# Two-layer hybrid diffusion block on one core: latent chains ahead of context chains, one convolution channel as fp32 diagonal products in idle stretches, two group norms at a time, a gradual weight split

## The chip, the cores and the metric

The kernel runs on one core of a Trainium2 chip. The metric is the device time of one execution in microseconds, median of three runs. The engines are TensorE (PE; PEld is its weight load), VectorE (DVE), ScalarE (ACT), GpSimd (POOL) and the queue that issues transfers (SP). Each engine works off its own queue in order; they meet by semaphores.

## The reference, cut to what matters

Two layers over 256 latent tokens of width 1024, with 256 context tokens in the first layer only. All of it is fp32.

```python
for i in range(2):
    x_lat = x_lat + 0.5 * post(swiglu(pre(x_lat, m, 0, g0), w_gu, w_down), m, 0, g1)
    if i == 0: x_ctx = the same for the context
    if i == 0:                                   # even mixer
        u = pre(x_lat, m, 1, g2) @ w_in
        a = silu(groupnorm(dw_conv31(u_a * sigmoid(u_g)) + b))     # 512 channels, 8 groups
        q, k, v = ...                            # 8 heads of 64
        b = softmax([q k_window + bias, q k_ctx]) @ [v_window, v_ctx]
        y = [a, b] @ w_out
    else:                                        # odd mixer
        b, c, z = split(pre(x_lat, m, 1, g2) @ w_in, 3)
        y = (b * dw_conv3(c * z)) @ w_out
    x_lat = x_lat + post(y, m, 1, g3)
    x_lat = x_lat + 0.5 * post(swiglu(pre(x_lat, m, 2, g4), w_gu2, w_down2), m, 2, g5)
pre(x, m, k, g)  = rms_norm(x, g) * (1 + m[3k+1]) + m[3k]
post(y, m, k, g) = m[3k+2] * rms_norm(y, g)
m = silu(c) @ w_mod + b                          # 9 rows of 1024 per layer
```

## The kernel before, in words

**Weights.** Every weight streams once through SBUF. A raw chunk arrives by one of SP's transfers (`load`, tile `wr`, four buffers), ACT rounds a piece of 128x512 to the TensorE's reduced fp32 (`cast`, the high half of `wx`), DVE subtracts for the low half (`feed`), and each product is three matmuls: high by high, high by low, low by high (`mm3`, `rows3`). A ring of 12 slots (`RING`), later 15, holds split pieces; some pages (`lent`) serve as further slots for the last products of a stage. `wtile` hands out a piece and splits `feedst["auto"]` pieces ahead: `LEAD` (6) as a rule and `DEEP` before a tail.

**Stages.** `ff1_0` works on latents and context together, 512 tokens wide, in five parts (`PARTS0`). The other feed-forward stages (`half_step` for `ff2_0`, `ff1_1`, `ff2_1`) work on 256 latents: 22 pairs of gate and up, 48 matmuls each, then the down projection in `Out`. Between them stand the even mixer (`ev_in`, `ev_out`) and the odd one (`od_in`, `od_out`).

**Order.** The queues are written out by hand: after `pin[0] = True` every instruction stays where it was emitted. A planner carries a clock for PE, DVE and ACT (`clk`, `cost_pe` and so on). Chains of work are generators started by `spawn`; each yields the clock at which it wants to go on, and `tick`, called with each weight piece, lets those that are due emit. `need(cond)` moves PE's clock on to the next due chain until the condition holds. `filler` emits weight splits, or taps of the convolution, where ACT or DVE is not far ahead of PE.

**Modulation rows.** DVE makes most of `m` as 128 rows of dot products (`mod_dot`, tile `junk`, one instruction each per condition); POOL loads each row (`mod_load`, tile `mr`) into one of three or four pages when the dot product before it has freed the page. `bg(n)` emits n of them.

**End of the first stage.** After each of four token tiles of the last down part a chain `chain0(t)` normalises the row, updates the residual, normalises again, transposes in four quarters on PE and splits the result in two halves for `ev_in` (`hla` for the latents t = 0 and 1, `hct` for the context t = 2 and 3). Each chain is started as soon as its tile is done.

**Even mixer.** `ev_in` makes four convolution channels tiles and q from the latents, then v of all tokens (waits for the context's chains), then k. The convolution's 31 taps run on DVE for channel tiles 0 to 2 (`taps`, tile `bufD`); tile 3 runs on PE as products with diagonal matrices in the split form, three matmuls a tap (`taps_pe`), each step of k followed by one tap (`next(tap_pe, None)`). POOL lays the diagonals (`lay`, two instructions a tap, a ring of four). `groups` normalises the tiles one after the other: matmuls for mean, variance and spread, and a power on POOL. `unit(n)` is one half of a pair of heads of the attention: scores, a bias that POOL has loaded and negated (`bias_load`, tile `bt`, DMA and multiply emitted together), softmax, transposes, and the product with v. `ev_out` takes its eight k tiles in `EV_ORDER`; the last four (`EV_TAIL`) form its tail.

**`Out`.** It accumulates two token tiles in four PSUM banks, leaves the last `tail` k tiles to the end, tile by tile, and for each token tile a `chain(t)` normalises, updates the residual, multiplies by the next scale row on POOL (`PO.tensor_mul`), normalises, transposes and splits into `hin`; `head` starts the next stage tile by tile while the other chain still runs. The chains of both tiles emit by due time; the first square of each is emitted right after its first bank.

## Time and profile before

| | before |
|---|---|
| median of three runs | 1312.34 us (1312.02 to 1313.12) |
| the profiled execution's own time | 1318.65 us |
| its span in the profile | 1316.9 us |
| PE busy | 1234.2 us (94%), 7321 matmul records |
| DVE / ACT / POOL busy | 884.8 / 583.8 / 181.5 us |
| mean granted TensorE clock | 0.966 |
| HBM | 259.74 MB read, 198 GB/s over the span |

The profile is of one execution. Busy time counts an engine's instructions as a union over time; PE at half its clock is busy for twice as long with the same work, so idle time and granted clock are read together. Fp32 matmuls show as two records each. All work of the pinned part has the line of the helper that emits it (L110), so groups are told apart by tiles.

### The profile page before, as it was taken

What the parts mean: (1) busy time and instruction counts of PE and PEld (TensorE: products, weight loads), DVE (VectorE), ACT (ScalarE), POOL (GpSimd) and SP (SyncE); (2) the same over time, 40 slices, a digit from 0 to 9 for tenths busy, and PEclk for the clock granted to TensorE, in tenths of its full rate; (3) what the DMA queues carried; (4) which work ended last, traced back from release to release, by engine and by line L of the source; (5) the groups of instructions that cost most, each with busy time, mean ns of one, the idle gap of its engine ahead of it and who ended that gap; (6) DMA issues with size and microseconds to landing.
All of it is one profiled execution on the core that took longest, in us unless ns stands there. A gap on an engine that the chain in (4) does not pass through costs nothing.

```text
span 1316.9 us, 19547 instructions
## 1 busy us (share of the span) xinstructions
PE 1234.2 (94%) x7321; PEld 1081.7 (82%) x7321; DVE 884.8 (67%) x1681; ACT 583.8 (44%) x1209; POOL 181.5 (14%) x273
## 2 busy tenths in 40 slices
PE   7999999999996978876999999999998899999997
PEld 4788888888875967754999987999987897899986
DVE  5868787776464765473677776677867687676562
ACT  5542323222357514453455455444545345454451
POOL 0001011211010046502000102100102001100000
PEclk9999999999996988997999999999998989999999
DMA  8846466885321611150588894678984467476670
GB/s 323 323 144 217 166 221 227 286 289 180 103 102 40 217 49 60 57 173 16 199 281 272 313 331 141 222 266 272 321 308 145 144 194 254 165 252 197 195 262 34
DMA packets 73895, 262.13 MB, mean 199 GB/s; under 512 B 8188, under 2 KB 10436, under 8 KB 73800
## 3 DMA queue, kind: packets, MB, share of 16 engines
q1 hardware_dynamic: 52440, 183.74, 40.4%
q0 software_dynamic: 21360, 77.14, 18.1%
q8 instruction: 57, 0.93, 0.3%
q14 instruction: 38, 0.31, 0.1%
HBM read 259.74 MB, written 1.11 MB: 198 GB/s over the span
## 4 chain that ended last, share of the span: by engine, by line
PE 42%; DVE 6%; DMA 6%; ACT 3%; issue 1%; POOL 0%; DVEq 0%; POOLq 0%; ACTq 0%; SPq 0%
PE mm L110 40%; DMA wr<-in_wflow 6%; DVE wx L110 2%; PE bc L110 2%; DVE junk L110 1%; DVE yw L110 1%; ACT wx L110 1%; ACT ajunk L110 1%; DVE xt L110 1%; DVE xn L110 0%; DVE gh L110 0%; DVE uu L110 0%; ACT hin L110 0%; DVE hin L110 0%; ACT gs L110 0%
## 5 line engine op out<-in xcount | busy, mean ns | idle before, releaser
L110 DVE TENSOR_TENSOR wx<-wr,wx 128x512 fp32r<-128x512 f32 x648 | 417.9, 691 | 76.0 <-ACT wx L110 75.7
L110 ACT CAST wx<-wr 128x512 fp32r<-128x512 f32 x648 | 365.6, 618 | 196.1 <-DMA wr<-in_wflow 141.8
L110 PE MATMUL mm<-hin,wx 128*128 128x256 f32 x3168 | 385.1, 284 | 3.6 <-DVE wx L110 3.6
L110 PEld LDWEIGHTS mm<-hin,wx 128*128 128x128 f32 x3168 | 383.6, 193 | 3.8 <-DVE wx L110 3.8
L110 PE MATMUL mm<-hh,wx 128*128 128x512 f32 x704 | 220.2, 392 | 1.8 <-ACT hh L673 1.3
L110 DVE SCALAR_TENSOR_TENSOR junk<-mr,cb 128x1024 bf16<-128x1024 f32 x156 | 190.0, 1218 | 0.3
L110 PEld LDWEIGHTS mm<-hh,wx 128*128 128x128 f32 x704 | 132.9, 189 | 30.5 <-ACT hh L673 1.8
L110 POOL DMA_DIRECT2D mr<-in_wmodb x128 | 69.0, 539 | 571.5 <-DVE junk L110 524.1
L110 PE MATMUL mm<-hl,wx 128*128 128x512 f32 x352 | 137.4, 390 | 0.0
L110 PE MATMUL mm<-wx,Hh 128*128 128x512 f32 x352 | 108.8, 390 | 0.0
L110 DVE TENSOR_TENSOR gh<-gs,mm 128x256 f32<-128x256 f32 (+2 forms) x93 | 43.7, 474 | 95.4 <-ACT gs L110 55.5
L110 ACT ACTIVATE gs<-mm 128x256 f32<-128x256 f32 (+2 forms) x91 | 38.7, 429 | 133.3 <-PE mm L110 133.3
L110 PE MATMUL mm<-wx,hin 128*128 128x256 f32 (+1 forms) x384 | 80.7, 363 | 7.4 <-ACT hin L110 6.3
L110 PEld LDWEIGHTS mm<-wx,hin 128*128 128x128 f32 x384 | 61.7, 201 | 19.5 <-ACT hin L110 8.3
L110 PEld LDWEIGHTS mm<-hl,wx 128*128 128x128 f32 x352 | 66.4, 189 | 13.7
L110 PEld LDWEIGHTS mm<-wx,Hh 128*128 128x128 f32 x352 | 65.8, 188 | 13.7 <-DVE wx L110 0.2
L110 PE MATMUL mm<-hla,wx 128*128 128x256 f32 x384 | 61.5, 307 | 12.7 <-ACT hla L110 11.8
L110 PEld LDWEIGHTS mm<-hla,wx 128*128 128x128 f32 x384 | 54.3, 207 | 18.2 <-ACT hla L110 13.3
L110 PE MATMUL mm<-wx,Hl 128*128 128x512 f32 x176 | 68.6, 390 | 0.0
L110 PE MATMUL mm<-wx,Hb 128*128 128x512 f32 x288 | 67.2, 389 | 0.0
L110 PEld LDWEIGHTS mm<-wx,Hb 128*128 128x128 f32 x288 | 54.1, 188 | 11.2
L110 ACT CAST Hh<-gh 128x512 fp32r<-128x512 f32 x22 | 13.6, 620 | 108.8 <-DVE gh L110 108.8
(195 smaller groups left out, 1195.4 us busy)
## 6 DMA issues: line engine op xcount, KB each, us to landing
wr<-in_wflow SPq DMA_DIRECT2D x324, 512.0 KB, 5.5
mr<-in_wmodb POOLq DMA_DIRECT2D x128, 512.0 KB, 5.7
mr<-in_wmoda SPq DMA_DIRECT2D x8, 512.0 KB, 8.3
wme<-in_wmoda SPq DMA_DIRECT2D x8, 512.0 KB, 7.7
pr<-rowh POOLq DMA_DIRECT2D x7, 512.0 KB, 8.9
xt<-in_xtok SPq DMA_DIRECT2D x4, 512.0 KB, 3.9
bt<-in_bias POOLq DMA_DIRECT2D x4, 512.0 KB, 4.1
pr<-rowev POOLq DMA_DIRECT2D x3, 512.0 KB, 3.8
```

The costliest lines, as they stand in the source:

```text
L110: ins = f(*a, **kw)
```

## The change

1. `chain0` of a context tile waits until both latent tiles are through; its first square is one instruction of 1024 and its scaled copy two of 512 in place of four of 256.
2. Channel tile 0 in place of 3 goes to PE, as one fp32 matmul a tap and one diagonal on POOL, in a ring of eight. The taps no longer stand in the k loop: `need` calls them when no chain is due within 0.3 of PE's planned clock. DVE has tiles 1 to 3. `EV_ORDER` has tile 1 in front of tile 0.
3. Two `groups` generators run side by side.
4. `bias_load` is a chain: the transfer, 7 later the negation in two halves; a unit does not begin before its bias is there. The first load is emitted ahead of the v products. The row `M0` for `ev_out` is asked for when channel 0 is done, and the tail waits for all three rows.
5. In `Out`, chain 1 begins when chain 0 has emitted its second multiply, squares are emitted when their bank is full by the planner, the second multiply goes from POOL to DVE, and the first two transposes share a step.
6. The split ahead of a tail grows from 7 to 22 pieces by one a step (before: 6, then 18 for the last four), with three more lent pages (`M1` to `M3`); in `od_in` it grows from 6 to 14. The 16 modulation rows done beside those products move to `ff1_0`.

```diff
...
 PARTS0 = (4, 4, 4, 5, 5)
-EV_ORDER = (6, 4, 5, 0, 1, 2, 3, 7)
+EV_ORDER = (6, 4, 5, 1, 0, 2, 3, 7)
 EV_TAIL = 4
 LEAD = 6
-DEEP = 18
+DEEP = 22
 BACK = 1.2
...
     filler = [None]
+    idle_pe = [None]
...
                 return
+            if idle_pe[0] and min(x[0] for x in tasks) > clk["pe"] + 0.3 and idle_pe[0]():
+                tick()
+                continue
             clk["pe"] = max(clk["pe"], min(x[0] for x in tasks))
...
-        def __init__(self, name, base, src, K, tail, rows_, out_t=None, fill=None, lend=4, dots=0):
+        def __init__(self, name, base, src, K, tail, rows_, out_t=None, fill=None, lend=("A0", "A1", "A2", "A3", "M1", "M2", "M3")):
             self.rows, self.out_t = rows_, out_t
                                                  (K - tail) * KD + (n * tail + k - K + tail) * 4), 4)
-            lent.update({first + n: f"A{n}" for n in range(lend)})
+            lent.update({first + n: tag for n, tag in enumerate(lend)})
             self.y = y = [[take() for _ in range(2)] for _ in range(2)]
             for k in range(K - tail):
-                feedst.update(hold=(offs[name] * NTILE + base + k * KD) // 4, auto=DEEP if k >= K - tail - 4 else LEAD)
+                feedst.update(hold=(offs[name] * NTILE + base + k * KD) // 4, auto=max(feedst["auto"], min(DEEP, DEEP + 1 - K + tail + k)))
                 for t in range(2):
                         rows3(y[t][n], src(k), k, TS[t], w(k, n), k == 0, False)
-                bg(1 if k % 2 == 0 and k // 2 < dots else 0)
             feedst["hold"] = first
             filler[0] = fill or more
-            need(lambda: self.rows)
+            need(lambda: len(self.rows) == (1 if out_t else 3))
+            self.filled, self.mark = [0, 0], 0
             for t in range(2):
-                gen = self.chain(t)
+                spawn(self.chain(t), True)
                 for n in range(2):
                         rows3(y[t][n], src(k), k, TS[t], w(k, n), False, k == K - 1)
-                    if n == 0:
-                        next(gen)
-                spawn(gen, True)
+                    self.filled[t] = n + 1
                 feedst.update(hold=None, auto=0, at=first)
...
             for n in range(2):
+                while self.filled[t] <= n or self.mark < t:
+                    yield clk["pe"] + 0.2
                 square(ss, n, y[n])
             r = rstd(ss)
+            if self.out_t is not None:
+                self.mark = 1
             yield clk["dv"] + POW
             for n in range(2):
-                PO.tensor_mul(yw[:, half(n)], x[:, half(n)], a[:, half(n)])
+                DV.tensor_mul(yw[:, half(n)], x[:, half(n)], a[:, half(n)])
+            self.mark = 1
             yield both() + 0.1
...
             for c0, c1 in ((0, 2), (2, 4), (4, 8)):
-                while not free:
+                while len(free) < (2 if c0 == 0 else 1):
                     yield clk["pe"] + 0.2
-                pt = take("bc")
-                for k in range(c0, c1):
-                    PE.transpose(pt[:, (k - c0) * P:(k - c0 + 1) * P], yw[:, k * P:(k + 1) * P], ident)
+                pts = [take("bc")] if c0 != 2 else pts[1:]
+                if c0 == 0:
+                    pts.append(take("bc"))
+                pt = pts[0]
+                for p, e0, e1 in ((pts[0], 0, 2), (pts[1], 2, 4)) if c0 == 0 else ((pt, 4, 8),) if c0 == 4 else ():
+                    for k in range(e0, e1):
+                        PE.transpose(p[:, (k - e0) * P:(k - e0 + 1) * P], yw[:, k * P:(k + 1) * P], ident)
                 pv = pt[:, :(c1 - c0) * P].rearrange("p (q t) -> p q t", t=P)
...
                 self.ready[t] = c1
-                yield clk["pe"] + 0.3
+                if c0 == 2:
+                    yield clk["pe"] + 0.3
...
                           ("M0", "Y2", "Y3")[:3 if pre else 1])
-        return Out(name, NF * 16, H, NF, TAIL, rs, out_t, dots=8)
+        return Out(name, NF * 16, H, NF, TAIL, rs, out_t)
...
     feed(feedst["at"] + 1 + LEAD)
-    mod_begin(24 + 32 + 8, ("M0", "M1", "M2", "M3"))
+    mod_begin(24 + 32 + 24, ("M0", "M1", "M2", "M3"))
     parts = PARTS0
...
         a, b = pre[t // 2]
+        while t > 1 and min(kq[:2]) < KD:
+            yield clk["pe"] + 0.2
         ss = small.tile([P, 2], F32, name="ss")
-        for n in range(2):
-            clk["ac"] = both()
-            square(ss, n, y[:, half(n)])
+        clk["ac"] = both()
+        square(ss, 0, y)
         for n in range(2):
         yield both() + 0.1
-        r = rstd(ss)
+        r = rstd(ss[:, 0:1])
         yield clk["dv"] + POW
         for n in range(4):
-            c = slice(n * S, (n + 1) * S)
-            AC.activation(y[:, c], x[:, c], AF.Copy, scale=r)
-            yield clk["ac"] + 0.1
+            if n % 2 == 0:
+                AC.activation(y[:, half(n // 2)], x[:, half(n // 2)], AF.Copy, scale=r)
+                yield clk["ac"] + 0.1
             while not free:
...
                             k == 0, k == KD - 1)
-                        nd = (4, 5, 5, 4, 4 if f < 2 else 0)[pi]
+                        nd = (4, 5, 5, 5, 2 if f < 2 else 0)[pi]
                         bg(((gu * KD + k + 1) * nd) // 16 - ((gu * KD + k) * nd) // 16)
...
                 give(y[n])
-            if not last:
-                bg(1)
+            if not last and t:
+                bg(2)
             if last:
...
     acc = bufD[:, 2048:3072].rearrange("p (c t) -> p c t", t=S)
-    av = big.tile([P, 3, PADW], F32, name="av", tag="F")
+    avs = [big.tile([P, n, PADW], F32, name="av", tag=tag) for n, tag in ((3, "F"), (1, "M0"))]
+    av = [avs[1][:, 0, :]] + [avs[0][:, i, :] for i in range(3)]
...
     def taps():
-        for i in range(3):
+        for i in range(1, CT):
             for d in range(TAPS):
                     yield False
-                src = av[:, i, d:d + S]
+                src = av[i][:, d:d + S]
                 if d == 0:
...
-    diag = big.tile([P, 4, 2, P], F32R, name="diag", tag="R12")
+    diag = big.tile([P, 8, P], F32, name="diag", tag="R12")
     laid = []
         if d < TAPS:
-            PO.tensor_scalar(diag[:, d % 4, 0, :], ident, taph[:, d:d + 1].bitcast(F32), None, op0=ALU.mult)
-            PO.tensor_scalar(diag[:, d % 4, 1, :], ident, tapl[:, d:d + 1], None, op0=ALU.mult)
-            laid.append(max(laid[-1] if laid else 0, clk["pe"]) + 1.0)
+            PO.tensor_scalar(diag[:, d % 8, :], ident, dwh[:, 0, d:d + 1], None, op0=ALU.mult)
+            laid.append(max(laid[-1] if laid else 0, clk["pe"]) + 0.8)
     def taps_pe():
-        for _ in range(4):
+
+        for _ in range(8):
             lay()
-        yield
         ps = take()
         for d in range(TAPS):
-            w = diag[:, d % 4]
-            for u, v in ((0, 0), (0, 1), (1, 0)):
-                PE.matmul(ps[:, :S], lhsT=w[:, u, :], rhs=avp[:, v, d:d + S], start=d + u + v == 0,
-                          stop=d == TAPS - 1 and u == 1, skip_group_check=True)
+            while laid[d] > clk["pe"]:
+                yield False
+            PE.matmul(ps[:, :S], lhsT=diag[:, d % 8, :], rhs=av[0][:, d:d + S], start=d == 0, stop=d == TAPS - 1)
             lay()
-            if d == TAPS - 1:
-                AC.activation(acc[:, 3, :], ps[:, :S], AF.Identity, bias=dv[:, 0, 3:4])
-                give(ps)
-                st_["conv"].add(3)
-            yield
+            yield True
+        AC.activation(acc[:, 0, :], ps[:, :S], AF.Identity, bias=dv[:, 0, 0:1])
+        give(ps)
+        st_["conv"].add(0)
...
-        for n in range(CT):
-            while not (st_["conv"] - normed) or not turned():
+        while len(normed) < CT:
+            if not (st_["conv"] - normed) or not turned():
                 yield clk["pe"] + 0.5
+                continue
             i = min(st_["conv"] - normed)
...
         i, t = divmod(n, 2)
-        while st_["k"] <= i or st_["begun"] < n or st_["done"] < n - 1 or len(free) < 2:
+        while i not in bts or st_["k"] <= i or st_["begun"] < n or st_["done"] < n - 1 or len(free) < 2:
             yield clk["pe"] + 0.2
...
         if t == 1 and i + 1 < CT:
-            bias_load(i + 1)
+            spawn(bias_load(i + 1))
         if t == 1 and i >= 2:
...
     def bias_load(i):
-        bts[i] = page("bt", f"M{2 + i % 2}", [P, 2, 2, S])
-        PO.dma_start(out=bts[i], in_=bias[i])
-        PO.tensor_scalar(bts[i], bts[i], -1.0, None, op0=ALU.mult)
+        bt = page("bt", f"M{2 + i % 2}", [P, 2, 2, S])
+        PO.dma_start(out=bt, in_=bias[i])
+        yield clk["pe"] + 7
+        for m in range(2):
+            PO.tensor_scalar(bt[:, m], bt[:, m], -1.0, None, op0=ALU.mult)
+            yield clk["pe"] + 1
+        bts[i] = bt
     filler[0] = mixer_fill
-    spawn(groups())
+    for _ in range(2):
+        spawn(groups())
     for i in range(CT):
...
         AC.activation(th, ps[:, S:], AF.Tanh, scale=0.5)
-        if i < 3:
-            DV.scalar_tensor_tensor(av[:, i, PADT:PADT + S], th, 1.0, ps[:, :S], op0=ALU.add, op1=ALU.mult)
-        else:
-            avp = page("avp", "M0", [P, 2, PADW], F32R)
-            pad(avp.bitcast(F32))
-            a2, (ah, al) = work.tile([P, S], F32, name="full"), (avp[:, u, PADT:PADT + S] for u in range(2))
-            DV.scalar_tensor_tensor(a2, th, 1.0, ps[:, :S], op0=ALU.add, op1=ALU.mult)
-            AC.copy(ah, a2)
-            DV.tensor_sub(al, a2, ah.bitcast(F32))
+        DV.scalar_tensor_tensor(av[i][:, PADT:PADT + S], th, 1.0, ps[:, :S], op0=ALU.add, op1=ALU.mult)
         give(ps)
...
         give(ps)
+    spawn(bias_load(0))
     for t in range(4):
...
     mixer_pages()
-    bias_load(0)
     for n in range(2 * CT):
...
                     k == 0 and v == 0, k == KD - 1, True)
-            next(tap_pe, None)
         AC.copy(kT[:, i, :], ps)
         give(ps)
+        idle_pe[0] = lambda: next(tap_pe, False)
         st_["k"] = i + 1
-    ev_rows.insert(0, row_of(ev_vec[0], 0, "M0"))
+    def first_row():
+        while 0 not in st_["conv"] or len(ev_rows) < 2:
+            yield clk["pe"] + 0.5
+        ev_rows.insert(0, row_of(ev_vec[0], 0, "M0"))
+
+    spawn(first_row())
-    post = Out("ev_out", 0, src, KD, EV_TAIL, ev_rows, None, mixer_fill, 3)
+    post = Out("ev_out", 0, src, KD, EV_TAIL, ev_rows, None, mixer_fill, ("A0", "A1", "A2"))
     slots[:0] = ["X2", "X3", "R12"]
-    post = half_step(post, "ff2_0", 0, 2, 27, (), (1, 0))
-    post = half_step(post, "ff1_1", 1, 0, 27, (), (1, 1))
+    post = half_step(post, "ff2_0", 0, 2, 19, (), (1, 0))
+    post = half_step(post, "ff1_1", 1, 0, 19, (), (1, 1))
...
     for j in range(2, KD):
+        feedst["auto"] = LEAD + max(0, j - 3) * 2
         pcx, pb = take(), take()
         for u, ps in enumerate(dst):
...
```

## Rows read from the trace of the kernel before

**Rows 1.** What PE waited for: us in total, times, longest.
```profile
PE mm L110 <- POOL diag L110: 13.1, 4, 6.3
PE bc L110 <- DVE yw L110: 12.1, 4, 4.3
PE mm L110 <- ACT hla L110: 11.8, 4, 6.2
PE mm L110 <- ACT hin L110: 6.3, 8, 3.0
```

**Rows 2.** Stretches: length, busy us (instructions) of five engines, PEclk, DMA share, GB/s.
```profile
60.00:340.00 280.00, 280.00 (x1237) 231.50 (x1236) 207.02 (x344) 85.25 (x153) 32.35 (x60) 1.00 0.64 214
...
394.00:452.00 58.00, 44.98 (x314) 42.02 (x315) 32.69 (x73) 40.11 (x97) 2.07 (x3) 0.82 0.34 108
...
476.00:600.00 124.00, 96.18 (x611) 78.77 (x609) 64.59 (x162) 52.03 (x115) 57.22 (x77) 0.87 0.26 85
600.00:632.00 32.00, 24.21 (x106) 19.57 (x107) 14.71 (x31) 12.81 (x31) 10.22 (x11) 0.85 0.18 60
```

**Rows 3.** The page's slices: granted TensorE clock in tenths, 40 slices of 33 us.
```profile
PEclk9999999999996988997999999999998989999999
```

**Rows 4.** PE in order of time, from the last down product to v: start, length.
```profile
392.54 0.40 PE L110 MATMUL mm<-wx,Hl 128*128 128x512 f32 x1
...
401.44 1.90 PE L110 MATMUL mm<-hla,wx 128*128 128x256 f32 x6 [6.23 <-ACT hla L110]
...
452.06 11.07 PE L110 MATMUL mm<-wx,hla 128*128 128x512 f32 x48
```

**Rows 5.** DVE and ACT in the latent chains, in order of time.
```profile
382.02 0.69 DVE L110 TENSOR_TENSOR yp<-mm,yp 128x512 f32<-128x512 f32 x1 [0.72 <-PE mm L110]
...
384.28 0.81 ACT L110 ACTIVATE xn<-bc,b,a 128x128 f32<-128x128 f32 x2 [1.80 <-PE bc L110]
...
385.12 0.41 ACT L110 CAST hla<-xn 128x256 fp32r<-128x256 f32 x1
```

**Rows 6.** PE's groups in three stretches: busy us, mean ns, idle before.
```profile
L110 PE MATMUL mm<-hin,wx 128*128 128x256 f32 x912 | 109.9, 283 | 0.0
...
L110 PE MATMUL mm<-wx,hla 128*128 128x512 f32 x48 | 11.1, 390 | 0.0
...
L110 PE MATMUL mm<-bufD,dgb 128*128 128x256 f32 x8 | 2.8, 427 | 4.2 <-DVE bufD L110 3.5 <-DVE dgb L110 0.7
```

**Rows 7.** POOL and PE at the mixer's first stall, in order of time.
```profile
480.21 2.79 POOL L110 TENSOR_SCALAR bt<-bt 128x1024 f32<-128x1024 f32 x1 [3.45 <-DMA bt<-in_bias]
...
483.63 1.16 PE L110 MATMUL mm<-avp,diag 128*128 128x256 f32 x3 [6.30 <-POOL diag L110]
```

**Rows 8.** DVE's last taps and PE's tail of `ev_out`, in order of time.
```profile
589.30 2.56 DVE L110 SCALAR_TENSOR_TENSOR bufD<-av,dwh,bufD 128x256 f32<-128x256 f32 x5
...
599.88 11.84 PE L110 MATMUL mm<-wx,mix 128*128 128x512 f32 x45 [2.56 <-ACT mix L110]
```

**Rows 9.** Groups: taps at 440 to 472 and 500 to 560, lays at 460 to 625.
```profile
L110 DVE SCALAR_TENSOR_TENSOR bufD<-av,dwh,bufD 128x256 f32<-128x256 f32 x35 | 16.9, 483 | 0.9
...
L110 DVE SCALAR_TENSOR_TENSOR bufD<-av,dwh,bufD 128x256 f32<-128x256 f32 x26 | 14.5, 558 | 0.7
...
L110 POOL TENSOR_SCALAR diag<-ident,taph 128x128 fp32r<-128x128 f32 x31 | 19.5, 630 | 7.8 <-PE mm L110 7.8
```

**Rows 10.** Ends of feed-forward stages: three engines in order of time, one stretch.
```profile
819.73 1.79 DVE L110 TENSOR_TENSOR wx<-wr,wx 128x512 fp32r<-128x512 f32 x1
...
1004.19 2.89 POOL L110 TENSOR_TENSOR yw<-xt,pr 128x512 f32<-128x512 f32 x2 [0.93 <-DVE xt L110]
...
1009.64 0.69 PE L110 MATMUL bc<-ident,yw 128*128 128x128 f32 x2 [3.88 <-DVE yw L110]
...
1012.00:1016.00 4.00, 4.00 (x18) 3.40 (x17) 0.71 (x2) 1.02 (x3) 0.00 (x0) 0.52 0.00 0
```

**Rows 11.** Modulation rows loaded at 60 to 340, from issue to landing.
```profile
DMA to landing us min/median/max: 3.8/5.0/8.5
```

23 lines of the change are left out of this document (11 added, 12 removed).

## The prediction, made before the change was run

> **What bounds the kernel now.** I read the page's slices first, then PE's waits, then the stretches one by one. PE is the bound: in long stretches it is busy all the time at full clock, as from 60 to 340 us (280.00 of 280) [rows 2]. So only stretches in which PE idles, or runs at a lower clock, can give time back without less work. The clock row shows where: dips at slices 12 and 13, around 20, at 32 and 34 [rows 3]. The list of waits gives the causes: 13.1 us for the diagonals that POOL lays, 12.1 us in four waits for `yw` (the ends of four stages), 11.8 us for `hla`, 6.3 us for `hin` [rows 1]. Three places follow.
>
> At 394 to 452, between the first stage and v, PE is busy 44.98 of 58 us at 0.82 of its clock; at 476 to 600, k, attention and convolution, 96.18 of 124 at 0.87; and four ends of stages, of which the one at 600 to 632 shows 24.21 of 32 at 0.85 [rows 2]. The reader should see in [rows 10] that an idle stretch costs twice: at 1012 to 1016 PE is busy for all 4 us, but at 0.52, the lower of its two levels (1.2 GHz), just after a wait of 3.88 us.
>
> **Part A, latent chains first.** PE ends the last down product at 392.54 + 0.40 = 392.9 and begins v at 452.06, 59.1 us later [rows 4]. Between lie 288 products of 256 columns (4 x 48 for the channels, 96 for q). One costs 109.9 / 912 = 0.1205 us in a full stretch [rows 6], so 34.7 us; the other 26 of the 314 PE records are transposes, at half a product each 1.6 us. What is left is the wait for `hla` and the low clock after it.
>
> When can the latents be ready? Token tile 1's sum is written at 382.02 + 0.69 = 382.7 [rows 5]. Tile 0 shows the length of a chain that met little else: its sum came 30 products of 512 columns earlier (11.1 / 48 = 0.23 us each [rows 6], so near 375.8), and its first quarter reached ACT at 384.28, 8.5 us later. Tile 1 then has its first quarter near 391.2; four quarters at ACT's 0.81 + 0.41 us [rows 5] end at 396.1. PE needs a quarter each 0.72 us from 392.9 on and the last at 395.1. I take 2.5 us of wait (bounds: none, and 8.5 as now, from 392.9 to 401.4). So 34.7 + 1.6 + 2.5 = 38.8 in place of 59.1: 20 us less (bounds 14 and 22). The context's chains now begin near 396; they need about as long as the latents' two, some 20 us, and v asks for them after 38.8 + 11 us. ACT's 40.11 of 58 us busy [rows 2] is the same work in less time, so this cover is thin: if it fails, v waits for some 5 us of it. That wait is also the one that the change adds: behind `chain0` of the context stand only the norms and v, and both are later.
>
> **Part C, the mixer.** From 476 to the end of `ev_out` at 599.88 + 11.84 = 611.7 [rows 8] it takes 135.7 us. Two things leave PE's path. The old taps: 93 products, 11.2 us. And POOL's block: the negation of the bias waits 3.45 us for its transfer and then runs 2.79, while PE's next tap stands 6.30 us for its diagonal [rows 7]; with three more such waits that is the 13.1 us [rows 1], and lower clock after each.
>
> What comes: 31 fp32 taps. The nearest fp32 products of this shape (`bufD,dgb`, two records each) show 2.8 / 4 = 0.70 us standing alone [rows 6]; two plain products would be 0.24. I take 0.45: 14 us (7 to 22), placed where the planner has PE idle. Units that poll come back each 0.2, under the 0.3 that the rule asks, so the taps start only when all eight units have begun; I expect most of them in the wait ahead of `ev_out`'s tail.
>
> What is late next is DVE: three channel tiles of 31 taps, as before. DVE is busy 64.59 us at 476 to 600 [rows 2]; with some 5 us more of early weight splits 70 us are owed. It worked 52% of that time because it stood behind the stalled PE; in the first stage, which it does not bound, it works 207 of 280 us, 74% [rows 2]. I take 78%, since while PE waits at the tail nothing stands in front of the taps: 90 us. Then follow a norm chain (from the last tap at 591.9 to 599.9, 8.0 us) and the tail (11.8) [rows 8]: 110 us, 26 less. The best case is PE's own work: 96.18 x 0.87 = 84 us at full clock, less 11 + plus 14, plus the tail: 98 us, 37 less. The worst is with the rivals. Two group norms at once keep a finished tile from waiting for another's chain; they are hidden behind the taps, and without that cover one chain of 8 us comes out. The first bias load, moved ahead of v, puts one transfer and one negation into a POOL that is busy 2.07 of 58 us there [rows 2]. A unit that waits for its bias is no longer emitted early, so PE has k products in front of it and not a stall; if k is used up, each of three later loads costs its 3.45 + 2.79 = 6.2 us, of which the other half of the pair hides most. The row for `M0`, now asked for after channel 0, lands behind that channel's own norm chain of 8 us. The new order of k tiles moves no product.
>
> Here a row speaks against the change: taps take 483 ns with POOL quiet and 558 while it lays diagonals [rows 9]. By the row the price is 50 taps x 0.075 = 4 us at most of DVE, inside my 78%. The Trainium skill, SBUF — State Buffer, section "Who interferes with whom", says more: a DVE instruction with two SBUF inputs and a GpSimd instruction that reads SBUF shut each other out for the whole instruction. A tap and a lay are such a pair. By that rule the sum would lose up to 19 us, by the row 4; I go by the row and keep the rule's result as a rival.
>
> **Parts D to G, four ends of stages.** At stake are 12.1 + 6.3 us of waits [rows 1] and the clock after them, some 2 us each time (4 us at 0.52 [rows 10]): 26 us. The chain of tile 0 loses POOL's multiply (2.89 us for two [rows 10]) for two DVE ones of 0.69 each, and the power behind it in POOL's queue; DVE and ACT no longer stand at tile 1's square while tile 0 could go on. I put tile 0's chain at 8 us from its last bank. Behind a feed-forward tail PE has 36 products of 512 columns, 8.3 us, of tile 1 to do, so nearly nothing is left; behind `ev_out` 24, 5.5 us, so 2.5 are left. Adding 1 us each for the other tile and some clock, 7 of the 26 us stay: 19 less (bounds 5 and 24). The POOL multiply also held DVE up: a split of 0.69 took 1.79 beside it [rows 10]; that goes too. The gradual split and the 16 rows taken from these stages save nothing by themselves, PE being full there; they keep ACT's and DVE's queues short at the ends.
>
> **The first stage** gets 16 more dot products of 1.3 us, 21 us of DVE, of which 280 - 207 = 73 us are free [rows 2]: nothing. If the cover were gone, all 21 us. Their 16 transfers go through POOL's queue, which has nothing else there, at a DMA share of 0.64 [rows 2].
>
> **Sum.** 20 + 26 + 19 = 65 us off the profiled execution's own 1318.65 (its span of 1316.9 and 1.75 around it): 1253.65. The median of the runs shown is 6.3 us under that execution, so 1247.
>
> **Rivals.** (1) DVE stays held up in the mixer, by POOL's 31 lays (31 x 0.63 = 19.5 us [rows 9]) or by waiting at instructions whose banks are late: PSUM holds four banks of `ev_out`, one of the taps, two of norms, so units wait for a pair. Part C gives 7 in place of 26: 1266. For it: taps 15% longer beside POOL; against it: half as many lays. (2) The taps don't fill idle time but the planner's idea of it: 14 us come onto PE's path: 1261. For it: this planner already missed POOL's 13.1 us; against it: PE was idle far longer in that stretch. (3) The ends of stages turn the wait over to DVE, which now does the multiply too: 5 in place of 19 us: 1261. For it: hin and yw waits both follow DVE; against it: those 1.4 us replace 2.9. (4) PE becomes the bound of the mixer, and ends come out best: 37 and 22: 1233. (5) Slower: the added rows in the first stage. With five dots in a pair of 48 products (11 us) each row that serves one dot has four pages' time, 8.9 us less issue and dot, some 7, to land; landings are 5.0 us in the median, 8.5 at most [rows 11]. A late row holds DVE's queue, behind it the splits, and then PE. Some 40 dots stand so close (in the fourth part, the end of the third, and the seven at once ahead of the context's rows). The change loses from the point where they use up DVE's 73 - 21 = 52 free us and the 65 gained: 117 / 40 = 2.9 us a dot, landings of 7 + 4 x 2.9 = 19 us. At 20 us of landing, 40 x 3.25 - 52 = 78 are lost against 65: 1325. Against it: the landings measured. (6) The change does not do what it says: each wait is replaced by a like one. The low bounds of A, C and the ends, the taps on the path and the context late, 14 + 7 - 14 + 5 - 5 = 7 us, and a part of the first stage's 21 uncovered: no change, 1312.
>
> **Chances.** Forecast 0.50 (its own range 1235 to 1258), (1) 0.18, (2) 0.09, (3) 0.09, (4) 0.07, (5) 0.04, (6) 0.03. The range 1232 to 1279 holds the forecast, the first three with some 10 us for two of them together, and most of the fourth; it leaves out (5) and (6). A measurement of this kernel can tell 0.2%, about 2.6 us: the first four and the forecast are faster, 0.93; within it lies (6), 0.03; slower (5), 0.04.
>
> **What would show it.** The first `hla` product should follow the last down product within some 3 us, with the clock at 1.00 there. PE's waits for `diag` and `hla` should be nearly gone and those for `yw` under 4 us. The fp32 taps should lie ahead of the tail of `ev_out`, and the last thing that the tail waits for should be DVE's tile 3. If PE waits for splits in the first stage, or `diag` is still in the list, or the stretch from v's end to the tail is over 125 us, I am wrong.

## The result and the profile after

The kernel after takes 1280.53 us, median of four runs (1278.25 to 1280.91), beside 1312.73 us (1312.02 to 1316.56) for the kernel before on the same chip: a ratio of 0.9745 (95% interval 0.9723 to 0.9768). It is faster, but by 32 us and not by 65. The profiled executions, on which the sum was made, stand at 1318.65 and 1280.91 us, 37.7 apart; the other 5.5 us are that the profiled execution of before lay 6 us above its median and that of after on it.

The page after, TensorE's busy time and the granted clock in 40 slices; in [rows 3] six slices lay under 9, here three do:

```profile
PE 1224.0 (96%) x7290; PEld 1071.1 (84%) x7290; DVE 887.8 (69%) x1694; ACT 580.7 (45%) x1192; POOL 145.3 (11%) x230
...
PEclk9999999999999999978999999999999998999999
```

TensorE's waits after (total, times, longest): against [rows 1] `diag` is gone and `hla` fell from 11.8 to 2.2, but `yw` only from 12.1 to 9.7, and waits for `mix`, `mixo` and `wx` have come in their place.

```profile
PE bc L110 <- DVE yw L110: 9.7, 5, 2.7
PE mm L110 <- DVE wx L110: 5.4, 6, 1.6
PE mm L110 <- ACT mix L110: 5.2, 2, 3.2
PE mm L110 <- ACT mixo L110: 3.4, 1, 3.4
...
PE mm L110 <- DVE bufD L110: 3.1, 1, 3.1
PE mm L110 <- ACT hla L110: 2.2, 2, 1.1
```

Cut at the same products in both traces, in us:

| stretch on TensorE | before | after | change | forecast |
|---|---|---|---|---|
| start to the last down product of `ff1_0` | 392.9 | 398.7 | +5.7 | 0 |
| from there to v (Part A) | 59.1 | 47.2 | -11.9 | -20 |
| v | 23.7 | 21.8 | -1.9 | 0 |
| k to the end of `ev_out` (Part C) | 136.0 | 117.7 | -18.3 | -26 |
| end of `ev_out` to the loop of `ff2_0` | 28.7 | 25.0 | -3.6 | |
| `ff2_0` to `ff1_1`, and `ff1_1` to `od_in` | 52.6 | 43.5 | -9.1 | |
| end of `od_out` to the loop of `ff2_1` | 25.2 | 25.8 | +0.6 | |
| (the four ends together) | 106.5 | 94.3 | -12.2 | -19 |
| loop of `od_in` and `od_out` | 81.3 | 82.0 | +0.7 | 0 |

The three long feed-forward loops with their down products are the same to 0.1 us. The sum is -37.8.

Part A after, the three stretches that hold its loss (columns as in [rows 2]): the clock is 0.77 behind two waits for `hla`, and at 426 ACT is full while TensorE is not.

```profile
398.70:404.60 5.90, 3.41 (x20) 2.50 (x20) 4.12 (x14) 5.78 (x15) 0.00 (x0) 1.00 0.11 36
404.60:412.00 7.40, 7.24 (x42) 6.80 (x43) 3.42 (x7) 3.78 (x9) 0.00 (x0) 0.77 0.33 115
...
426.00:436.00 10.00, 7.56 (x62) 7.15 (x61) 4.56 (x10) 9.81 (x25) 3.80 (x3) 1.00 0.46 164
```

The end of the mixer, which answers to [rows 8]: DVE's last taps, then TensorE's norm chain and tail, in order of time; then two stretches of it, columns as before.

```profile
556.46 4.88 DVE L110 SCALAR_TENSOR_TENSOR bufD<-av,dwh,bufD 128x256 f32<-128x256 f32 x9
```
```profile
555.66 2.75 PE L110 MATMUL mm<-av,diag 128*128 128x256 f32 x10
561.49 2.04 PE L110 MATMUL mm<-bufD,dgb 128*128 128x256 f32 x4 [3.08 <-DVE bufD L110]
...
571.55 13.88 PE L110 MATMUL mm<-wx,mix 128*128 128x512 f32 x48 [3.20 <-ACT mix L110]
588.15 1.09 PE L110 MATMUL bc<-ident,yw 128*128 128x128 f32 x4 [2.72 <-DVE yw L110]
```
```profile
560.00:564.00 4.00, 2.40 (x5) 1.53 (x6) 3.31 (x7) 0.42 (x1) 0.00 (x0) 0.54 0.53 180
...
572.00:576.00 4.00, 4.00 (x11) 3.03 (x11) 0.00 (x0) 0.00 (x0) 0.00 (x0) 0.50 0.00 0
```

TensorE stands from 558.4 to 561.5, the clock falls to its lower level (1.2 GHz) and stays there through both norms and 5.7 us of the tail: 48 products take 13.88 us.

### The profile page after: what moved, and what is told of

It reads as the page before. It is cut to its first block, busy times and chain, and to the rows that moved or that the text cites. A ratio compares the mean times of both kernels' runs of the same rounds, so it can differ in the third digit from the quotient of the medians.

```text
span 1279.1 us, 19477 instructions
## 1 busy us (share of the span) xinstructions
PE 1224.0 (96%) x7290; PEld 1071.1 (84%) x7290; DVE 887.8 (69%) x1694; ACT 580.7 (45%) x1192; POOL 145.3 (11%) x230
## 4 chain that ended last, share of the span: by engine, by line
PE 50%; DVE 4%; ACT 2%; DMA 1%; issue 1%; POOL 0%; DVEq 0%; POOLq 0%; ACTq 0%; SPq 0%
PE mm L110 49%; DMA wr<-in_wflow 1%; DVE bufD L110 1%; DVE xn L110 1%; PE bc L110 1%; ACT wx L110 1%; DVE wx L110 0%; ACT ajunk L110 0%; DVE yw L110 0%; DVE xt L110 0%; ACT hin L110 0%; ACT mixo L110 0%; DVE zp L110 0%; ACT mix L110 0%; ACT full L110 0%
## 5 line engine op out<-in xcount | busy, mean ns | idle before, releaser
L110 DVE TENSOR_TENSOR wx<-wr,wx 128x512 fp32r<-128x512 f32 x648 | 412.7, 686 | 84.2 <-ACT wx L110 84.0
L110 ACT CAST wx<-wr 128x512 fp32r<-128x512 f32 x648 | 366.0, 618 | 174.9 <-DMA wr<-in_wflow 124.3
L110 PE MATMUL mm<-wx,hin 128*128 128x256 f32 (+1 forms) x384 | 75.2, 353 | 2.1 <-DVE wx L110 1.1
L110 ACT CAST Hh<-gh 128x512 fp32r<-128x512 f32 x22 | 13.6, 620 | 122.6 <-DVE gh L110 122.6
L110 PEld LDWEIGHTS mm<-wx,Hb 128*128 128x128 f32 x288 | 54.1, 188 | 11.2
L110 POOL TENSOR_TENSOR rr<-uu,nhalf 128x1 f32<-128x1 f32 x26 | 21.5, 830 | 361.7 <-DVE uu L110 359.5
L110 PE MATMUL mm<-hla,wx 128*128 128x256 f32 x384 | 56.9, 293 | 5.6 <-DVE wx L110 2.9
```

Of the source, the lines that this page charges most:

```text
L110: ins = f(*a, **kw)
```

## The experiments

Each was timed beside the kernel before in three rounds (the last two in five); times are to be read against 1280.5. "Mixer" is from the end of v to the end of `ev_out`, 117.6 us after; the six traces in which nothing of it was changed (after, x1, x2, x3, x12, x14) give 116.3 to 119.0. A single trace is therefore read against that spread, and the clock is a part of it: the same instructions behind the same waits found it at 1.00 in one trace and lower in another (see Part A and the ends).

### The first stage, the order of the chains, the norms, the shift

**x2_rows_back**: the 16 rows go back to the stages they came from, with their dot products.

```diff
-mod_begin(24 + 32 + 24, ("M0", ...          # first stage
+mod_begin(24 + 32 + 8, ("M0", ...
-half_step(post, "ff2_0", 0, 2, 19, ...      # and ff1_1
+half_step(post, "ff2_0", 0, 2, 27, ...
-lend=("A0", "A1", "A2", "A3", "M1", "M2", "M3")
+lend=("A0", "A1", "A2", "A3")
```


> The 16 modulation rows go back beside the down products of ff2_0 and ff1_1, with the old numbers of dots a step, and pages M1 to M3 are no longer lent to weights; the gradual split stays. Theory (rows land late): the wait of DVE for mr in the first stage (6.4 us) and PE's small waits there (0.7 for Hh, 1.4 for vecs) go; the last down product ends 2 to 3 us earlier than 398.7 and the time is 1278. Rival (the first stage is longer because of its start, where PE ran at its lower clock): it ends at 398 within 1 us on a start like the last one, and the time is 1281 to 1284, since the ends of stages lose three pages.

1277.75 us (1276.74 to 1279.17), ratio 0.9712 (0.9681 to 0.9742). From the end of the first part (100.4 after, 101.1 here) to the last down product it took 295.1 us, as in the kernel before (294.9); after it takes 298.3. The mechanism is in the trace of after, DVE and then TensorE in order of time: a row 0.95 us late, `gh` behind it in DVE's queue, and TensorE late for `Hh`; a later wait of 1.4 us for `vecs` is of the same kind. In this experiment TensorE waits for nothing between 100 and 396 us. The other traces agree: this stretch takes 296.8 to 301.8 us in the fourteen that have all the rows in `ff1_0`, and 295.1 or 295.2 in the three that don't (x2, x15, x17).

```profile
286.39 1.22 DVE L110 SCALAR_TENSOR_TENSOR junk<-mr,cb 128x1024 bf16<-128x1024 f32 x1 [0.95 <-DMA mr<-in_wmodb]
287.55 0.08 DVE L110 DVE_READ_ACCUMULATOR junk<-mr,cb 128x1 f32 x1
287.55 0.68 DVE L110 TENSOR_TENSOR gh<-gs,mm 128x512 f32<-128x512 f32 x1
```
```profile
288.93 0.73 PE L110 MATMUL mm<-wx,Hh 128*128 128x512 f32 x2 [0.72 <-ACT Hh L110]
```

The other 2.4 us of the stage's 5.7 lie before 100 us, where traces of the same code there end between 97.3 and 101.1: a difference between executions.

**x3_ctx_free**: the context's chains are no longer held back.

```diff
-        while t > 1 and min(kq[:2]) < KD:
-            yield clk["pe"] + 0.2
```


> The context's chains are no longer held back behind the latents. Theory (the order is what part A gained): from the last down product to the first product of v it takes 57 to 59 us again in place of 47.2, with a wait for hla of some 6 us and half clock behind it: 1290 to 1292. Rival (the gain comes from the fewer and longer squares and copies on ACT): 48 to 51 us, 1281 to 1284.

1282.3 us (1281.74 to 1283.47), ratio 0.975 (0.9724 to 0.9776). Part A is 3.2 us longer (50.4) and the mixer 1.4, the waits for `hla` 3.2 in place of 2.2. My theory (1290 to 1292) fell: of Part A's gain of 11.9 the ranking itself is the smaller share, and its size is open, since with the ranking Part A takes 45.7 to 48.7 us, by what the clock did. The rest (fewer and longer squares and copies on ACT) was not taken apart.

**x7_one_norm**: one generator of norms in place of two (`for _ in range(2): spawn(groups())` becomes one `spawn`).

> One group-norm generator in place of two. Theory (tiles 0 and 3 finish their taps within 3 us of each other, so two chains side by side save one): the tail of ev_out begins 6 to 8 us later, 1287 to 1289. Rival (the two chains share DVE, ACT and a PE at half clock, so that they save little): 1 to 3 us later, 1282 to 1284.

1281.79 us (1277.81 to 1291.18), ratio 0.9755 (0.9708 to 0.9802). In its profile the mixer is 121.1, 3.5 longer; the median can't tell the kernels apart.

**x1_shift_first**: tile 1's second square and multiply wait until tile 0's shift has been emitted.

```diff
-                while self.filled[t] <= n or self.mark < t:
+                while self.filled[t] <= n or self.mark < t * (n + 1):
```


> In Out the second square of token tile 1 is emitted only after the shift of tile 0 (the scalar_tensor_tensor on yw). Theory (order on DVE): in the changed kernel that shift stands in DVE's queue behind tile 1's second multiply, which waits for PE's last bank, so PE waits 1.96 us at each feed-forward end and 2.7 us behind ev_out. Then PE's waits for yw fall from 9.7 to about 2 us, with half a us of clock each time: 6 to 9 us less than 1280.5, 1272 to 1275. Rival (the chain is too long in itself, or tile 1 pays it back at its own head): 1279 to 1281, with a new wait in front of tile 1's products.

1286.33 us (1283.08 to 1288.74), ratio 0.9778 (0.9748 to 0.9808): missed, the wrong way. At `ff2_0`'s end the wait for tile 0 fell from 1.96 to 1.16 us, and tile 1, which had not waited, waited 1.09; at `ev_out`'s end four weight splits (2.49 us) slipped into DVE's queue ahead of the shift, and that stretch took 29.2 in place of 25.0.

### The mixer

**x4_cut_dve, x5_cut_pe, x6_cut_both**: 8 taps in place of 31 for tile 3 on DVE, for tile 0 on TensorE, and for both.

```diff
-            for d in range(TAPS):
+            for d in range(TAPS if i < 3 else 8):   # x4; x5: range(8) in taps_pe, and no further lay()
```


> Leaves out 23 of the 31 taps of channel tile 3 on DVE (8 stay), 23 x 0.53 = 12 us of DVE in the mixer; all else as after. The kernel after takes 1280.5; there the last DVE tap ends at 561.3 and the last fp32 tap of TensorE at 558.4, both just before the two last group norms. Theory (the mixer's end is bound by DVE's taps, TensorE stands idle beside them): most of the 12 us comes off, 1270 to 1273. Rival (TensorE's own products with its 31 taps reach to 558.4, 3 us before DVE's end): no more than about 3 us comes off, 1277 to 1279, and the wait ahead of the first norm product goes.

> Leaves out 23 of the 31 fp32 taps of channel tile 0 on TensorE (8 stay), 23 products of 256 columns at some 0.28 to 0.43 us, 6 to 10 us of TensorE; DVE's taps as after. Theory (DVE bound, 561.3): nothing or at most 1 us, 1279.5 to 1281. Rival (the taps stand on TensorE's path because they come only behind the products of the first ev_out tiles, 538.7 to 558.4): 5 to 9 us less, 1272 to 1276.

> Leaves out 23 of the 31 taps of channel tile 3 on DVE and 23 of the 31 fp32 taps of tile 0 on TensorE. Alone they gave 5.1 us (4.7 in the mixer) and 1.7 us (2.6 in the mixer). Theory (both ends at 558 to 561, each hides what the other gives back): together 10 to 14 us less than after, 1267 to 1271. Rival (what is left is set by k, attention and the norms' chain, not by taps at all): about the sum of the two, 1273 to 1275.

x4 1275.46 us (1272.77 to 1276.85), mixer 112.9; x5 1278.83 (1273.66 to 1280.87), mixer 114.9; x6 1270.54 (1261.99 to 1274.42), mixer 105.4. So in the mixer 4.7 and 2.7 alone, 12.2 together (x6's profile is its fastest execution, by 7 us); by the medians 5.1, 1.7 and 10.0. In x4 TensorE's own taps still end at 557.8, in x5 DVE's at 559.9. Either hides most of the other, though x4's 4.7 is more than the 3 that the rival allowed.

**x16_eager**: DVE's taps may run further ahead.

```diff
-    return more(5) or (clk["dv"] < clk["pe"] + BACK and next(tap, False)) or more()
+    return more(5) or (clk["dv"] < clk["pe"] + 4 and next(tap, False)) or more()
```


> The planner may run DVE's taps 4 us ahead of TensorE's clock in the mixer (1.2 in the kernel after); all else as after (1280.5), nothing is left out. In the kernel after DVE is busy 12.0, 12.4 and 14.5 of 20 us in 480 to 540 and 17.8 in 540 to 560, where the last 32 taps stand. Theory (the taps' order in DVE's queue, not DVE's speed, makes the last tap end at 561): last DVE tap before 550, the mixer then ends by TensorE's taps and norms, 2.5 to 5 us less: 1275.5 to 1278. Rival (taps ahead in the queue delay the DVE steps that TensorE and ACT wait for, in attention above all): 1281 to 1286.

1288.42 us (1279.65 to 1291.38), ratio 0.9792 (0.9755 to 0.9829). DVE's last tap, then TensorE's last taps, in order of time; the stretch has the columns of [rows 2]:

```profile
523.89 1.51 DVE L110 SCALAR_TENSOR_TENSOR bufD<-av,dwh,bufD 128x256 f32<-128x256 f32 x3
```
```profile
560.16 11.05 PE L110 MATMUL mm<-av,diag 128*128 128x256 f32 x42
```
```profile
555.00:575.00 20.00, 16.22 (x78) 9.94 (x76) 3.97 (x10) 4.08 (x9) 15.95 (x25) 0.97 0.30 100
```

DVE is done 36 us sooner, and the mixer takes 117.2: nothing. TensorE's 21 last taps go at 0.53 us each while POOL, which lays their diagonals, is the busiest engine (15.95 of 20 us), and end at 571.2. The taps ahead of the splits cost the stretches before: Part A 49.6, v 24.6, the waits for `wx` 10.1 us. So DVE is not what bounds the mixer alone; both theory and forecast had it so.

**x10_taps_in_k**: one fp32 tap behind each step of k again.

```diff
                 mm3(ps[:, v * S:(v + 1) * S], ...)
+            next(tap_pe, None)
```


> The 31 fp32 taps are called after each step of k again, as in the kernel before, and in idle stretches behind that; all else as after (1280.5). In the kernel after they stand between 538.7 and 558.4 us, DVE's last tap ends at 561.3. Theory (the place of the taps matters little: they cost TensorE the same wherever they stand, and DVE's 561.3 sets the norms; what idle stretches were worth shows as the difference): 1280 to 1284. Rival (the idle stretches are what the change gained in the mixer): the taps push k and ev_out's first tiles back by 31 x 0.28 = 8 us and the time comes back to 1286 to 1289. Rival 2 (they stand too late in the kernel after, on the path of the last norms): 1275 to 1278.

1292.98 us (1291.07 to 1294.73), ratio 0.9832 (0.9812 to 0.9852), mixer 127.1. The first rival holds, and goes further than its 1286 to 1289: placement in idle stretches is worth 9.5 us of the mixer's gain. The taps in k are not simply added: `ev_out` starts 7 us later, two waits grow (those of this stretch), and DVE's last tap ends at 574.3 in place of 561.3:

```profile
PE mm L110 <- ACT gh L110: 9.1, 1, 9.1
PE mm L110 <- ACT mix L110: 8.2, 2, 5.7
```

**x9_warm**: TensorE is kept going with products that nobody reads, 14 behind the last tap and 12 behind the last spread.

```diff
+    def beat(n):
+        for _ in range(n):
+            PE.matmul(warm[0][:, S:S + P], lhsT=ident, rhs=mean, start=True, stop=True)
```


> 14 products of 128 columns in fp32 that nobody reads behind the last fp32 tap, and 12 behind the last spread of the two group norms, so that TensorE does not stand still from 558.5 to 561.5 and from 568.4 to 571.6; nothing is left out. In the kernel after the granted clock is 0.50 from 561 to 577 us, and the first half of ev_out's last 48 products runs at it. Theory (the standstill costs the clock, and the clock costs the tail): granted clock 1.0 from 558 to 585, the 13.88 us of the tail become 10.9 to 11.2, the norms' own products lose 1 to 2 us: 1275.5 to 1277.5. Rival (the clock falls anyway, or the chain of DVE, ACT and POOL sets the norms' length and the products only queue in front of it): 1280 to 1283.

1276.03 us (1274.58 to 1276.62), ratio 0.9707 (0.9682 to 0.9732): the theory, in size too. TensorE in order of time and one stretch:

```profile
559.41 1.03 PE L110 MATMUL mm<-bufD,dgb 128*128 128x256 f32 x4
...
567.91 11.21 PE L110 MATMUL mm<-wx,mix 128*128 128x512 f32 x48 [0.32 <-ACT mix L110]
```
```profile
568.00:572.00 4.00, 4.00 (x18) 3.21 (x19) 0.60 (x2) 0.69 (x2) 0.00 (x0) 1.00 0.02 4
```

The norms take 8.5 us from their first product to the tail (10.1 after), the tail 11.21 (13.88): mixer 113.1, 4.5 less. This does not hang on one trace: the tail has a mean clock of 0.77 to 0.88 in all fourteen traces of changed kernels without such products, and 1.00 in all five with them, where it takes 11.2 us (x9, x15, x17, x18, x19).

### Part A

**x11_warm_a** (such products, six ahead of the first and six ahead of the fifth tile of the latents) and **x13_ctx_raw** (the context's chains without scale and shift):

```diff
+                if i == 0 and u == 0 and k in (0, 4):
+                    for _ in range(6):
+                        PE.matmul(warm[:, :P], lhsT=ident, rhs=mean, start=True, stop=True)
```


> Six products of 128 columns in fp32 that nobody reads ahead of the first product on the latents and six ahead of its fifth tile, where the kernel after waits for hla twice (idle from 399.5 to 400.6 and 403.5 to 404.6) and shows a granted clock of 0.77 from 404.6 to 412; nothing is left out. Theory (those waits cost the clock, some 1.7 us, beside their own 2.5 us): 1.5 to 2 us less, 1278 to 1279, clock 1.0 from 404 to 412. Rival (the dummies stand in front of the products when hla is there, or ACT, not TensorE, sets this stretch and weight rounding waits take what is gained): 1280 to 1282.

> Leaves out the scale and shift of the context's two chains ahead of v (16 ACT operations of 128 columns, 0.40 us each, 6.5 us of ACT between 425 and 438), which copy from PSUM at once. In the kernel after ACT is busy 9.81 of 10 us in 426 to 436 and TensorE waits there 2.4 us for wx. Theory (ACT is the thin cover: the context's chains push the weights' rounding back): those waits go, 2 to 3 us less from the last down product to v (47.2 to 44.5), 1277.5 to 1279. Rival (the weights come late from their own order or from DMA): the waits stay, 1280 to 1281.5.

x11: 1284.18 us (1282.3 to 1286.07), Part A 45.6 with the clock at 1.00 throughout 398 to 430: 1.7 less, as expected in size. But it is no evidence for the unread products: Part A is 45.7 at a clock of 1.00 also in x1, x4, x6, x18 and x19, which have the two waits for `hla` and none of these products. What the traces show is the price of the clock. The same 98 products behind the same wait, in after and in x4:

```profile
404.61 14.29 PE L110 MATMUL mm<-hla,wx 128*128 128x256 f32 x98 [1.12 <-ACT hla L110]
```
```profile
405.01 12.78 PE L110 MATMUL mm<-hla,wx 128*128 128x256 f32 x98 [1.11 <-ACT hla L110]
```

That is 1.5 us; what decides whether the clock falls behind these waits stays open.

x13: 1282.25 us (1274.39 to 1285.6), Part A 42.4 at a clock of 1.00, so 3.3 less than the 45.7 at that clock (4.8 less than after), with 0.5 us of waits for `wx` in it (2.9 after). Its stretch at 426:

```profile
426.00:436.00 10.00, 10.00 (x86) 10.00 (x86) 7.42 (x14) 7.03 (x16) 3.04 (x2) 1.00 0.53 170
```

So x13 shows ACT's part, and it does not pay in the whole: the mixer is 122.2 in x11 and 124.3 in x13, 4.7 and 6.8 more. The taps fell otherwise (TensorE's last at 566 and 563), and in x13 3.3 us pass between v and k, most of it a wait of 2.6 for DVE. What of this is the order and what is chance stays open.

### The ends

**x12_warm_ends**: such products behind the last product of `ev_out` (11) and of `od_out` (8).

> Behind the last product of ev_out 11 and behind that of od_out 8 products of 128 columns in fp32 that nobody reads, at some 0.24 us each, in TensorE's wait for yw (2.72 and 1.96 us); nothing is left out. In the kernel after the granted clock is 0.50 at 588 to 592 and 0.69 to 596, and 0.64 at 1078 to 1082; behind the same 1.96 us of wait at the ends of ff2_0 and ff1_1 it is 1.00. Theory (the two ends that gained little, 3.6 us and -0.6 us, lose to the clock what the chain gives): 2.5 to 4.5 us less, 1276 to 1278, the stretch from ev_out's end to ff2_0's loop 22 to 23 in place of 25.0. Rival (ACT's and DVE's chain of tile 1, not the clock, sets these ends): less than 1 us, 1279.5 to 1281.

1281.38 us (1273.41 to 1288.81), ratio 0.9743 (0.9695 to 0.9792). The clock is 1.00 from 588 to 600, and tile 0's products end 2.6 us sooner behind `ev_out`'s end than after. Yet this end is no shorter (25.7): the time comes back at tile 1, in TensorE's order.

```profile
602.29 0.90 PE L110 MATMUL bc<-ident,yw 128*128 128x128 f32 x4 [1.50 <-DVE yw L110]
```

The cause stands in DVE's queue. Tile 1's shift (on `yw`) now comes behind the next stage's first product `gh`, which waits for ACT; after, it stands ahead of it, at 598.69. DVE in order of time, in x12:

```profile
601.23 0.62 DVE L110 TENSOR_TENSOR gh<-gs,mm 128x256 f32<-128x256 f32 x2 [0.95 <-ACT gs L110]
601.76 1.54 DVE L110 SCALAR_TENSOR_TENSOR yw<-yw,rr,pr 128x256 f32<-128x256 f32 x3
```

So an order that moved took the gain, and not a chain of tile 1 that was as late in itself, as the rival has it. Where the order stayed, this end goes with the clock of its first 15 us: 24.9 to 25.1 us long at 0.77 (seven traces, after among them), 23.9 to 24.0 at 0.89 (nine), and 22.9 at 1.00 in x16. The two ends between feed-forward and `od_in`, where they have the code of after, do the same: 21.7 to 21.8 us at 1.00, 23.2 to 23.4 at 0.86. `od_out`'s end gained 0.9. In this profile, the slowest of its executions, the wait for `mixo` is 6.1 us, 3.4 after.

**x14_od_split**: in `od_in` six pieces of lead again.

```diff
-        feedst["auto"] = LEAD + max(0, j - 3) * 2
+        feedst["auto"] = LEAD
```


> The gradual lead of the weight splits in od_in is undone (six pieces ahead throughout, as in the kernel before); all else as after. There ACT stands at 1057.4 behind 4.5 us of waiting for a weight from DMA, and the copy of the last short convolution behind it at 1057.9, so that TensorE waits 3.41 us for mixo at 1061.5 and runs at a granted clock of 0.57 after it. Theory (the larger lead moved the wait from wx to mixo): the mixo wait goes, and a wait of 1 to 4 us for wx may come back; 1278 to 1281. Rival (the larger lead is what shortens od_out's end): 1283 to 1286.

1274.23 us (1272.99 to 1277.4), ratio 0.9687 (0.9665 to 0.9709): better than the theory. In the kernel after, ACT and then TensorE in order of time:

```profile
1057.41 0.62 ACT L110 CAST wx<-wr 128x512 fp32r<-128x512 f32 x1 [4.50 <-DMA wr<-in_wflow]
1057.93 0.37 ACT L110 COPY full<-mm 128x256 f32<-128x256 f32 x1
```
```profile
1061.52 14.81 PE L110 MATMUL mm<-wx,mixo 128*128 128x512 f32 x57 [3.41 <-ACT mixo L110]
```

The copy that begins the last short convolution stands behind a rounding whose weight has not landed. In all fourteen traces with the larger lead TensorE waits 1.7 to 6.1 us for `mixo`, in the five with six pieces (x14, x15, x17, x18, x19) not at all. In x14 the 96 products run without a gap:

```profile
1050.61 21.95 PE L110 MATMUL mm<-wx,mixo 128*128 128x512 f32 x96
1077.15 1.10 PE L110 MATMUL bc<-ident,yw 128*128 128x128 f32 x4 [4.59 <-DVE yw L110]
```

### Together

**x15_best** (x2, x9 and x14), **x17_best_eager** (x16 too), **x18_half_rows** (x15, but rows back and fewer lent buffers at `ff2_0` alone) and **x19_od_beat** (x18 with 18 products that nobody reads behind `od_out`):

```diff
+        lend = ("A0", "A1", "A2", "A3") + (() if name == "ff2_0" else ("M1", "M2", "M3"))   # x18
+            beats = {"od_out": 18}.get(name, 0)                                             # x19
```


> Three edits that were run alone, together: the rows of the modulation back beside the last products of ff2_0 and ff1_1 (2.8 us alone), products that nobody reads in TensorE's idle stretches of the last norms (4.5), six pieces of lead in od_in (6.3). Nothing is left out. Theory (three places that don't touch each other): the sum, 13.6 off 1280.5, 1265 to 1269. Rival (they share DVE's queue and the weights' order, so that the wait shows elsewhere): 1270 to 1275.

> As x15_best with DVE's taps 4 us ahead of TensorE's clock. Theory: with the norms' clock kept, DVE's earlier end shows in full, 2 to 5 us below x15_best. Rival (TensorE's taps hold the same end): the same as x15_best within 1 us, or slower by the attention's waits, up to 5 us.

> As x15_best, but the rows of the modulation go back beside the last products of ff2_0 alone (8 of 16), and the last products of ff1_1 lend all seven buffers to the weights again. x15_best takes 1271.3. Theory (the 3.6 us of wait for wx in od_in come from the three buffers not lent at the end of ff1_1): that wait goes, the first stage loses 1 to 2 us of the 3 again: 1268 to 1270. Rival (the wait comes from DMA or DVE's queue and stays): 1272 to 1273.

> As x18_half_rows, with 18 products of 128 columns in fp32 that nobody reads behind the last product of od_out, some 4.3 us, in TensorE's wait of 4.6 us for yw there (x14). Theory (the wait costs the clock: x14 shows 0.65 at 1076 to 1080 and 0.92 at 1080 to 1084): 1 to 2 us below x18_half_rows. Rival (as in x12_warm_ends at ev_out's end, the chain of tile 1 then makes TensorE wait for what it gained): the same within 0.5 us.

x15 1271.34 us (1270.03 to 1274.24), ratio 0.967 (0.9654 to 0.9686): 9.2 of the 13.6. TensorE waits 3.6 us in `od_in`, as in x2:

```profile
1010.94 23.82 PE L110 MATMUL mm<-hin,wx 128*128 128x256 f32 x184 [3.60 <-DVE wx L110]
```

x17 1284.78 (1278.12 to 1287.2): the rival's slower branch, and beyond its 5 us. x18 1271.17 (1267.36 to 1272.76): the wait is gone (the loop of `od_in` 54.9 in place of 58.3), the median no lower than x15's. Rows and lent buffers moved together in x18, so which of the two made the wait is not shown. x19 1268.74 (1265.87 to 1271.76), ratio 0.9652 (0.9631 to 0.9673): `od_out`'s end 24.3 in place of 25.9, the clock behind it 1.00 in place of 0.77 (first 15 us). It beats both kernels, 11.8 us below the kernel after by the medians; from x18 its times can't be told apart.

## Why the prediction was wrong

The direction and most of the mechanisms stood; every gain in the sum was too large, and the first stage and the gradual split, put at nothing, cost time. Of the signs that the prediction named, the one that spoke against it was the wait for `yw`: 9.7 us, where under 4 were expected. In terms of the profiled executions the kernel after should have come at 1253.65 and came at 1280.91. The 27.3 us:

- **Part A, 8.1.** "38.8 in place of 59.1" took the products at full clock and 2.5 us of wait. The wait came as taken (1.12 twice, and the issue gaps about them). PE is busy 41.5 us where I had 36.3, and this was the larger error: 1.5 of it is the lower clock, as at 404 to 412 (40.0 in x4 and x6, at 1.00 throughout), and 3.7 is the price of a product, taken from a full stretch: here 98 products take 12.78 us at full clock, 0.13 each where I took 0.1205, and the transposes come on top. Why they are dearer here is open. PE also stands 2.9 us for `wx`, at 419 to 436: the thin cover, which the text named and priced at 5 us, then left out of the sum. x13, which spares ACT, takes 3.3 back at the same clock.
- **Part C, 7.7.** The removed parts are gone, and idle stretches were the right place (x10). 90 us for DVE's taps became 93.6. "A norm chain (8.0) and the tail (11.8)" became 10.1 and 13.9, because TensorE stands ahead of the chain and the clock drops; with the clock kept they are 8.5 and 11.2 (x9). That is 4.2 of the 7.7. The step's claim that DVE alone is "late next" fell in x16: DVE, TensorE's fp32 taps with POOL's diagonals, and the products themselves end within 3 us of each other. The price of a tap was right (14.8 us for 31, 0.48 each, where I took 0.45). What each removed part, the bias chain above all, is worth alone was not run.
- **Parts D to G, 6.8.** "DVE and ACT no longer stand at tile 1's square" is half true: a wait of 1.96 us stands at both feed-forward ends (before: 1.96 and 3.88), because tile 0's shift still comes behind tile 1's second multiply. The two ends between feed-forward and `od_in` gave 9.1 us, from the smaller waits for `hin` and `yw` and the clock; up to 1.6 of it is this trace's luck, which found the clock at 1.00 at both, while eight of the twelve other traces with the same code there show 0.86 at one. TensorE, in order of time:

```profile
782.64 0.83 PE L110 MATMUL bc<-ident,yw 128*128 128x128 f32 x4 [1.96 <-DVE yw L110]
```

  x1 shows that this wait is not what an end costs: taken off tile 0 it appears at tile 1. The end of `ev_out` gave 3.6 us; with the clock at 1.00 it would have given 5.8 (22.9 in x16). That of `od_out` gave none.
- **The gradual split, valued at nothing, 0.7 by the table.** Two halves hide in it. The loop of `od_in` became 4.6 us shorter (54.8, before 59.3; 58.2 in x2, whose last products have the rows and four lent pages), and `od_out` 5.3 longer, since the larger lead in `od_in` filled ACT's queue with roundings that wait for DMA, and the short convolution stood behind them: about 5 us from `od_in`'s loop to the loop of `ff2_1` (107.8 after, 102.8 in x14). In `od_in` "keep ACT's and DVE's queues short" was the opposite of what it does.
- **The first stage, 5.7.** Rival 5's mechanism was there on a small scale: late rows hold DVE and then TensorE, some 3.3 us; the rest is not the change's.
- v gave 1.9 us that had not been forecast. Multiplying on DVE in place of POOL was not tried alone, so its share is open.

Of the rivals the first was nearest in number (1266) and wrong in cause: a tap beside POOL's lays takes 511 ns, 484 without (DVE's and POOL's groups at 538 to 560, against [rows 9]):

```profile
L110 DVE SCALAR_TENSOR_TENSOR bufD<-av,dwh,bufD 128x256 f32<-128x256 f32 x34 | 17.4, 511 | 1.0
```
```profile
L110 POOL TENSOR_SCALAR diag<-ident,dwh 128x128 f32<-128x128 f32 x23 | 14.2, 633 | 10.6 <-PE mm L110 10.6
```

That is 34 x 0.027 = 0.9 us. x5 says the same: with 23 of the 31 lays gone DVE's last tap ends 93.8 us behind v, 93.5 after. The Trainium skill, SBUF — State Buffer, section "Who interferes with whom", would have such a pair shut each other out for whole instructions, 19 us by the forecast's count; this trace does not agree for taps and lays. It shows a loss on POOL's side elsewhere: the first eight lays ran beside DVE's weight splits and took 1.07 us each, while the splits kept 0.67. POOL, then DVE, in order of time:

```profile
521.87 8.53 POOL L110 TENSOR_SCALAR diag<-ident,dwh 128x128 f32<-128x128 f32 x8
```
```profile
522.80 5.33 DVE L110 TENSOR_TENSOR wx<-wr,wx 128x512 fp32r<-128x512 f32 x8
```

## What to carry to other kernels

Price a removed wait at the row where the next engine is late, and price the stretch behind the wait that is left at the clock that such waits already show: the clock cost 4 us in one place here. One trace of each kernel is not enough for a step of 1 or 2 us: look for the same stretch, with the same code, in the traces of the other experiments. Splitting weights further ahead is not free where their engine also has the next stage's chain: what stands in an in-order queue behind a transfer is late by the transfer. When several engines end together, taking one away shows little; take two away in one run before naming a bound.

## What the runs showed of the hardware

Behind a stop of 3.1 us TensorE was at its lower clock, and behind a second one of 3.2 us the tail ran 13.88 us; 26 unread products of 128 columns in fp32, 0.24 us each, kept it at 1.00 and the tail at 11.21. The clock also differs between traces of the same code: behind two waits of 1.12 us it was 0.77 over the next 7.4 us in after and 1.00 in x4, 98 products taking 14.29 and 12.78 us, and `ev_out`'s end took 25.0, 24.0 or 22.9 us at 0.77, 0.89 or 1.00. Moving DVE's last tap 36 us changed the mixer's length by 0.4 us. Executions of one kernel spread by 2 us (x9) to 15 us (x12); the clock is one part of it, the rest was not tried.
